# A chunked delta-rule scan: the first inversion's input copied in two parts, the scans' output matmuls split another way

## The chip, the cores and the metric

The kernel runs on one NeuronCore of a Trainium2 chip. TensorE (PE) multiplies matrices out of SBUF into PSUM banks; VectorE (DVE), ScalarE (ACT) and GpSimd (POOL) work elementwise; SyncE (SP) and ScalarE issue the DMAs. Each engine runs its own instructions in a fixed order and waits on semaphores for the others. The metric is device microseconds of one execution; the median of three runs counts.

## The reference

The model is a trunk of two layers over 512 positions of 1024 channels in float32, each followed by a gated convolutional FFN. Layer 0 is a spatial-gating MLP, layer 1 an RWKV-7 time mixer with 16 heads of 64 channels. The change lies in the time mixer. Its core is a recurrence per head:

```python
def step(state, inp):
    r_t, w_t, k_t, v_t, a_t, b_t = inp
    sa = jnp.einsum('bhvk,bhk->bhv', state, a_t)
    state = (state * w_t[:, :, None, :]
             + sa[..., None] * b_t[:, :, None, :]
             + v_t[..., None] * k_t[:, :, None, :])
    y_t = jnp.einsum('bhvk,bhk->bhv', state, r_t)
    return state, y_t
...
y = wkv7_scan(r_h, decay, k_h, v_h, -kk, kk * a_h)
mean = jnp.mean(y, -1, keepdims=True)
var = jnp.mean(jnp.square(y - mean), -1, keepdims=True)
y = ((y - mean) * lax.rsqrt(var + GN_EPS)).reshape(B, S, D)
y = y * ln_w.astype(f32) + ln_b.astype(f32)
bonus = jnp.sum(r_h * k_h * r_k.astype(f32), -1, keepdims=True) * v_h
return ((y + bonus.reshape(B, S, D)) * g) @ w_o
```

## The kernel before

The whole kernel is one program: the gating MLP, an FFN, the time mixer, an FFN, a final norm. Dense products are three float32r matmuls of 128x128 by 128x512 each (high by high, high by low, low by high; `mm3`, lines 325 to 327). The change touches only the time mixer, `rwkv_main`.

The recurrence is not run step by step. The 512 positions are cut in 8 chunks of 64. Heads go in pairs, two heads of 64 channels on 128 partitions: 8 pairs, in two groups `g` of four. Three kinds of work are chained:

**Pairs** (`pairs`, `decay`, `operands`, `products`). For pair `p` they work out decays and scaled operands and the 64x64 matrices of every chunk. Of these, `a` and `r` (tile `ar`) and the masked products (tile `lq`: a strictly lower one, M, and an inclusive one, N, per head) are stored by DMA in a DRAM buffer `std[g]`, laid out per chunk as 128 partitions by pair by RW = 320 columns. Before, the columns are `r` (0 to 64), then for head 0 first the block [a; M] and then N (64 to 192), and the same for head 1 (192 to 320); the store of `ar` takes three DMAs per pair on SP's queue, that of `lq` three per half. A further product is copied into `ti[g]`: the triangular matrices to be inverted.

**Inversions** (`invert(g)`). For a group the 32 unit triangular matrices (4 pairs by 8 chunks) of both heads are inverted at once in blocks of 32. Their input `x` is copied from `ti[g]` by quarter (`Q`), transposed by VectorE (`turn`, line 1051), eliminated in 30 steps on VectorE (lines 1058 to 1072), transposed back, and finished by small matmuls (lines 1090 and 1093). For `g == 0` the copy is four ScalarE copies of 32 partitions by all 1024 elements (line 1046) when pairs 0 to 3 are done. For `g == 1` it is ScalarE copies of 24 of the 32 matrices (line 1046) at one step and VectorE copies of the last 8 (line 1044) at the next.

**Scans** (`scan(g)`). For each chunk `c`, with tile `vu` holding the values `v` in one half of the partitions and the state in the other, a chunk has three parts, and yields after each:

- part A: the right side `us` = [a; M] by [state; v] (line 1301, 128 rows), copied to `wt` (line 1304); the first half of the output `e`, `r` by the state (line 1305, 64 rows); the decayed state `s0` on GpSimd;
- part B: the solve, `ti` by `wt` (line 1314, 64 rows), copied over the state's half of `vu` (lines 1315 and 1316);
- part C: the next state's product (line 1321, 128 rows, not in the last chunk), added to `s0` into the next chunk's `vu` (line 1325); the second half of the output, N by [solution; v] (line 1326, 128 rows), then two ScalarE copies of `e` into `y` (line 1329).

After every second chunk `finish` is started: it is the head norm of 128 positions (squares, a sum, a reciprocal root with GpSimd's power, a product, four transposes, line 1363, and a scaling on VectorE, line 1366). It is a generator, stepped once in each part (`self.step(late)`); what is left of it is drained (`yield from late`) before the next one takes its place. The last one of a scan is handed on (`left`).

`weave` sets the order around it. It steps a main generator (pairs, later a scan), and with each of its yields adds a rate to a sum; each time the sum reaches 1 it takes one step of `fill`: dense products of the projections, the gates and the output projection (`project`), two of its operands in a step. The rates are in `RATES` on line 33, 0.66 for the first scan and 0.72 for the second. A second generator, the inversion, is stepped beside. `issue_after` queues instructions of an engine behind a given one; within these limits a planner with its own cost model sets each engine's order.

After the second scan comes its end: the last `finish`, with steps of `fill` written out between its steps:

```python
rest, left = left.pop(), None
next(rest)
for _ in range(2):
    next(fill)
next(rest)
next(fill)
next(rest)
with tc.issue_after(self.last(mybir.EngineType.PE)):
    next(fill)
```

There `project` for group 1 gives no work until the last `finish` has gated its outputs.

## Time and profile before

| what | us |
|---|---|
| median of 3 runs | 1244.65 (1244.2 to 1246.1) |
| the profiled execution | 1245.55 |
| its span | 1243.7 |
| TensorE busy | 1226.8 (99%) |
| VectorE busy | 851.1 (68%) |
| ScalarE busy | 633.1 (51%) |
| GpSimd busy | 81.4 (7%) |
| mean granted TensorE clock | 0.996 of full speed |

The times of the profile are those of one execution. A row of a timeline gives the start in us from the span's beginning, the busy time, engine, line, operation, the tiles written and read, the shape, and the number of instructions that were merged in the row; in brackets the idle time of the engine just before and what ended it. Matmuls are pipelined: the time that a batch takes of TensorE is the distance of its start to the next one's start. The pairs run from about 570 to 720 us, the scans from 725 to 845 us.

### The profile page before, as it was taken

How to read it: one execution, taken by the hardware profiler on the slowest of the kernel's cores; microseconds unless marked ns; L12 is line 12 of the kernel's file. 1: busy time of each engine (PE TensorE's matmuls, PEld its weight loads, DVE VectorE, ACT ScalarE, POOL GpSimd, SP SyncE). 2: the span in 40 equal slices, each digit the busy share in tenths (PEclk: the TensorE clock that was granted, in tenths of full speed). 3: DMA queues.
4: the chain of work that ended last, by engine and by line, in shares of the span. 5: the costliest groups of instructions: out<-in, count | busy, mean ns of one | idle time of the engine just before them, and what ended most of it. 6: DMA issues, size and time to landing. Idle time of an engine off the chain costs nothing.

```text
span 1243.7 us, 19411 instructions
## 1 busy us (share of the span) xinstructions
PE 1226.8 (99%) x7535; PEld 1000.2 (80%) x7535; DVE 851.1 (68%) x1418; ACT 633.1 (51%) x1089; POOL 81.4 (7%) x106
## 2 busy tenths in 40 slices
PE   9999999999999999999999999999999999999997
PEld 6878888888888888877887777778888888888886
DVE  5566578888876454675899698776777777872323
ACT  6544455555554343466787667424544444543232
POOL 1100200000000001000000013222000000000000
PEclk9999999999999999999999899999999999999999
DMA  7232457887556776326888797654223223333332
GB/s 273 94 105 82 132 180 246 246 249 241 192 172 193 220 226 196 109 81 182 220 242 237 188 280 233 219 171 135 85 102 102 90 97 102 97 88 104 97 93 81
DMA packets 125133, 201.65 MB, mean 162 GB/s; under 512 B 39857, under 2 KB 63153, under 8 KB 125041
## 3 DMA queue, kind: packets, MB, share of 16 engines
q10 hardware_dynamic: 38976, 112.87, 29.5%
q1 hardware_dynamic: 86064, 87.54, 22.6%
q8 instruction: 59, 0.97, 0.3%
q14 instruction: 34, 0.27, 0.1%
HBM read 152.93 MB, written 47.45 MB: 161 GB/s over the span
## 4 chain that ended last, share of the span: by engine, by line
PE 91%; DVE 4%; DMA 3%; ACT 1%; issue 0%; SPq 0%; POOL 0%; DVEq 0%; POOLq 0%; ACTq 0%
PE mm L325 9%; PE mm L327 9%; PE mm L326 9%; PE aux L325 6%; PE aux L326 6%; PE aux L327 6%; PE e L325 6%; PE e L326 6%; PE us L325 6%; PE e L327 6%; PE us L327 6%; PE us L326 6%; PE us L1314 1%; PE aux L973 1%; PE aux L988 1%; PE us L1321 1%
## 5 line engine op out<-in xcount | busy, mean ns | idle before, releaser
L237 ACT CAST w<-w 128x512 fp32r<-128x512 f32 x340 | 206.5, 611 | 359.8 <-PE aux L327 92.6
L238 DVE TENSOR_TENSOR w<-w,w 128x512 fp32r<-128x512 f32 x340 | 230.5, 680 | 180.2 <-ACT w L237 179.6
L325 PE MATMUL mm<-mxh,w 128*128 128x512 f32 x408 | 167.9, 412 | 2.7 <-DVE rt L885 2.6
L327 PE MATMUL mm<-mxh,w 128*128 128x512 f32 x408 | 161.1, 395 | 0.0
L326 PE MATMUL mm<-mxl,w 128*128 128x512 f32 x408 | 160.6, 394 | 0.0
L325 PEld LDWEIGHTS mm<-mxh,w 128*128 128x128 f32 x408 | 77.0, 189 | 22.8 <-DVE rt L885 3.3
L327 PEld LDWEIGHTS mm<-mxh,w 128*128 128x128 f32 x408 | 77.0, 189 | 17.1 <-issue 0.8
L326 PEld LDWEIGHTS mm<-mxl,w 128*128 128x128 f32 x408 | 77.1, 189 | 16.2 <-issue 1.7
L575 ACT ACTIVATE cv<-z,par 128x512 f32<-128x512 f32 x88 | 71.7, 817 | 26.5 <-DVE z L573 21.2
L325 PE MATMUL aux<-mxh,w 128*128 128x512 f32 x216 | 84.5, 391 | 0.0
L325 PE MATMUL us<-mxh,w 128*128 128x512 f32 x216 | 84.5, 391 | 0.0
L327 PE MATMUL aux<-mxh,w 128*128 128x512 f32 x216 | 84.2, 390 | 0.0
L326 PE MATMUL aux<-mxl,w 128*128 128x512 f32 x216 | 84.1, 389 | 0.0
L326 PE MATMUL us<-mxl,w 128*128 128x512 f32 x216 | 84.1, 389 | 0.0
L327 PE MATMUL us<-mxh,w 128*128 128x512 f32 x216 | 84.1, 389 | 0.0
L354 POOL TENSOR_TENSOR ss<-ss,sq 128x512 f32<-128x512 f32 x24 | 31.7, 1323 | 761.1 <-ACT sq L352 761.1
L325 PE MATMUL e<-mxh,w 128*128 128x512 f32 x208 | 81.4, 391 | 0.0
L326 PE MATMUL e<-mxl,w 128*128 128x512 f32 x208 | 81.1, 390 | 0.0
L327 PE MATMUL e<-mxh,w 128*128 128x512 f32 x208 | 81.0, 389 | 0.0
L576 DVE SCALAR_TENSOR_TENSOR cv<-z,par,cv 128x512 f32<-128x512 f32 x88 | 66.0, 752 | 19.5 <-ACT cv L575 19.5
L577 DVE SCALAR_TENSOR_TENSOR cv<-z,par,cv 128x512 f32<-128x512 f32 x88 | 66.0, 752 | 2.9
L325 PEld LDWEIGHTS aux<-mxh,w 128*128 128x128 f32 x216 | 40.5, 188 | 9.0 <-issue 0.5
(1113 smaller groups left out, 2555.2 us busy)
## 6 DMA issues: line engine op xcount, KB each, us to landing
w<-in_wup ACTq DMA_DIRECT2D x88, 512.0 KB, 3.7
w<-in_wdn ACTq DMA_DIRECT2D x32, 512.0 KB, 3.7
st<-std SPq DMA_DIRECT2D x15, 640.0 KB, 6.6
w<-wkd ACTq DMA_DIRECT2D x16, 512.0 KB, 5.1
w<-wvd ACTq DMA_DIRECT2D x16, 512.0 KB, 5.1
w<-wod ACTq DMA_DIRECT2D x16, 512.0 KB, 4.2
w<-in_wdn ACTq DMA_DIRECT2D x16, 384.0 KB, 3.3
w<-in_wsu ACTq DMA_DIRECT2D x8, 512.0 KB, 3.7
```

The lines of the kernel that those rows point to most:

```text
L237: nc.scalar.copy(hi[r, :n], src)
L238: (lo_eng or nc.vector).tensor_tensor(lo[r, :n], src, hi[r, :n].bitcast(F32), ALU.subtract)
L325: mm(acc, wh, xh, start=first, stop=False)
L326: mm(acc, wh, xl, start=False, stop=False)
L327: mm(acc, wl, xh, start=False, stop=last)
L354: nc.gpsimd.tensor_tensor(self.ss, self.ss, self.sq, ALU.add)
L575: nc.scalar.activation(c, z[:, 2:], AF.Identity, scale=cw(2, i), bias=self.p("conv_b", l * 44 + i))
L576: nc.vector.scalar_tensor_tensor(c, z[:, 1:T + 1], cw(1, i), c, ALU.mult, ALU.add)
L577: nc.vector.scalar_tensor_tensor(c, z[:, 0:T], cw(0, i), c, ALU.mult, ALU.add)
L973: nc.tensor.matmul(qs[hd][:, c - ch.start, :], bk[H[hd], c, C * hd:C * hd + P], ar[H[hd], c, :], start=True, stop=True)
L988: nc.tensor.matmul(qs[hd][:, c, :], bk[H[hd], c, C * hd:C * hd + P], dg[H[hd], c, :], start=True, stop=True)
L1314: nc.tensor.matmul((us, ux)[hd][H[hd], 1, i, :], ti[g][H[hd], i, c, :], wt[H[hd], i, :], start=True, stop=True)
```

## The change

Three things are changed, all of them in `rwkv_main`.

**The input of the first inversion.** The split of the second inversion (24 matrices by ScalarE, then 8 by VectorE) is used for both. The first inversion is created before the pairs' first weave, and its first step (the ScalarE copies of the matrices of pairs 0 to 2) is taken as soon as pair 2 is done, from inside that weave (`opened`). Its second step (VectorE's copies, the transpose) comes where the whole copy stood.

**The output's halves.** `e` is now first [r; N] by [state; v] (128 rows, `both(i, hd, 1)`), in part A, and then N by the solution (64 rows), in `ready`. `ready` is called in part B of the next chunk, behind the solve's copies and queued behind the solve's matmuls, or at once in the last chunk. Its ScalarE copies into `y` go with it. For that, `std` has another layout: `r` stands in the rows of `a`, and N's columns of the solution's rows stand at 0 to 64. `ar` is stored in two DMAs of 128 columns instead of three of 64.

**The norms.** Since `y` is complete one chunk later, `finish` for two chunks starts in part B of the chunk after the next pair's begin, and the last but one is drained after the scan's last chunk.

```diff
-            for rows, o, q in ((h0, C, 0), (h1, 3 * C, 0), (slice(0, P), 0, C)):
-                nc.sync.dma_start(std[g][:, rows, i, o:o + C].rearrange("c p t -> p c t"), ar[rows, :, q:q + C])
+            for rows, o in ((h0, 3 * C), (h1, C)):
+                nc.sync.dma_start(std[g][:, rows, i, o:o + P].rearrange("c p t -> p c t"), ar[rows])
...
-                for hd, o, n, q in ((0, P, P + C, C), (1, C, P, 0), (1, 2 * P, C, P + C)):
+                for hd, o, n, q in ((0, 0, P + C, C), (1, 3 * C, P, 0), (1, 0, C, P + C)):
...
-            cut = 24 * g
-            for us in (slice(0, cut), slice(cut, 32))[1 - g:]:
+            for us in (slice(0, 24), slice(24, 32)):
                 for rows, cols in Q:
-                    if us.start and g == 1:
+                    if us.start:
                         V.tensor_copy(x[rows, us], tg[rows, us, cols])
                     else:
                         S.copy(x[rows, us], tg[rows, us, cols])
-                if g == 1 and us.start == 0:
+                if us.start == 0:
                     yield
...
-            y = None
+            y = past = ready = None
...
                 def both(i, hd, n):
-                    o = C + P * hd + n * C
+                    o = C + P * (1 - hd) + n * C
                     return st[i][:, o:o + C]
...
-                batch(lambda i, hd, n: nc.tensor.matmul(e[H[hd], 0, i, :], st[i][H[hd], 0:C], vu[H[hd], hd, i, :],
+                batch(lambda i, hd, n: nc.tensor.matmul(e[H[hd], 0, i, :], both(i, hd, 1), vu[:, hd, i, :],
                                                         start=i == 0, stop=False, skip_group_check=True), lead)
...
                 V.tensor_copy(vu[h0, 0], us[h0, 1])
                 S.copy(vu[h1, 1], ux[h1, 1])
+                if ready is not None:
+                    ready(self.last(mybir.EngineType.PE))
                 self.step(late)
+                if c % 2 == 0 and ready is not None:
+                    yield from late
+                    late = finish(g, c // 2 - 1, past)
                 yield
...
-                batch(lambda i, hd, n: nc.tensor.matmul(e[H[hd], 0, i, :], both(i, hd, 1), vu[:, hd, i, :],
-                                                        start=False, stop=True, skip_group_check=True), lead)
-                for hd in range(2):
-                    S.copy(y[H[c % 2], :, hd, :], e[H[hd], 0])
+
+                def ready(lead, c=c, e=e, st=st, vu=vu, y=y):
+                    batch(lambda i, hd, n: nc.tensor.matmul(e[H[hd], 0, i, :], st[i][H[hd], 0:C], vu[H[hd], hd, i, :],
+                                                            start=False, stop=True, skip_group_check=True), lead)
+                    for hd in range(2):
+                        S.copy(y[H[c % 2], :, hd, :], e[H[hd], 0])
+
+                past = y
+                if last:
+                    ready(None)
                 self.step(late)
                 yield
-                if c % 2 == 1:
-                    yield from late
-                    late = finish(g, c // 2, y)
-            left.append(late)
+            yield from late
+            left.append(finish(g, c // 2, y))
...
-        self.weave(until(main, lambda: 3 in done), None, fill, *RATES[0], ktiles=STEPS[0])
         inv = invert(0)
+
+        def opened(gen):
+            for _ in gen:
+                if 2 in done and not begun:
+                    begun.append(next(inv))
+                yield
+
+        begun = []
+        self.weave(opened(until(main, lambda: 3 in done)), None, fill, *RATES[0], ktiles=STEPS[0])
```

## The prediction

> **What bounds the kernel now.** I read the page first, then a table by stretches, then the timelines of single engines. The page:
>
> ```profile
> span 1243.7 us, 19411 instructions
> PE 1226.8 (99%) x7535; PEld 1000.2 (80%) x7535; DVE 851.1 (68%) x1418; ACT 633.1 (51%) x1089; POOL 81.4 (7%) x106
> ...
> PEclk9999999999999999999999899999999999999999
> ...
> PE 91%; DVE 4%; DMA 3%; ACT 1%; issue 0%; SPq 0%; POOL 0%; DVEq 0%; POOLq 0%; ACTq 0%
> ```
>
> TensorE is busy for all but 1243.7 − 1226.8 = 16.9 us, and the change neither adds nor removes a matmul. So time can come only from four places: idle TensorE, a slower granted clock, bubbles between matmuls of different shape, and new idle time. The clock row has one digit below nine, around 690 to 720 us. Cut finer (columns: stretch, its length, busy PE, PEld, DVE, ACT, POOL with counts, granted clock, DMA share, GB/s):
>
> ```profile
> 694.00:697.00 3.00, 0.72 (x5) 0.25 (x3) 2.83 (x10) 1.42 (x4) 0.00 (x0) 1.00 0.91 222
> ...
> 698.00:700.00 2.00, 1.81 (x15) 1.27 (x15) 2.00 (x2) 0.89 (x2) 0.00 (x0) 0.50 0.60 181
> 700.00:705.00 5.00, 5.00 (x44) 4.31 (x40) 1.48 (x1) 3.41 (x6) 0.00 (x0) 0.52 0.09 33
> ```
>
> TensorE idles 2.28 us in the first stretch and then runs at half clock; that loses about 2.0 × 0.50 + 5.0 × 0.48 = 3.4 us. The TensorE timeline gives the gap and its releaser:
>
> ```profile
> 694.31 0.40 PE L327 MATMUL mm<-mxh,w 128*128 128x512 f32 x1
> 696.99 0.50 PE L325 MATMUL mm<-mxh,w 128*128 128x512 f32 x1 [2.28 <-DVE rt L885]
> ```
>
> It waited for a VectorE instruction of line 885. VectorE's timeline shows what that one queued behind:
>
> ```profile
> 652.57 1.22 DVE L911 TENSOR_TENSOR_SCAN sq<-cst,sq 128x512 f32<-128x512 f32 x1
> 656.56 2.02 DVE L1051 STREAM_TRANSPOSE li<-ix 128x1024 f32<-128x1024 f32 x1 [2.77 <-ACT ix L1046]
> ...
> 696.25 0.68 DVE L885 TENSOR_TENSOR rt<-mm,v 128x512 f32<-128x512 f32 x1
> ...
> 714.75 1.18 DVE L1044 COPY ix<-ti 32x256 f32<-32x256 f32 x4
> ```
>
> Between the transpose at 656.56 and line 885 no row of this timeline carries an idle time: VectorE is the bound of that stretch, and it enters it 2.77 us late because ScalarE copies the first inversion's input (ix).
>
> **Part 1, the early copy.** The 2.77 us hole goes if three quarters of the copy are made earlier. In their place VectorE gets four copies of 32x256, which the second inversion already has: 1.18 us. Net −1.6 us for everything behind VectorE. But ScalarE must make four copies of 32x768 one pair earlier, and these are priced by the second inversion's as well (grouped by line; the second pair of numbers is busy us and mean ns):
>
> ```profile
> L1046 ACT COPY ix<-ti 32x768 f32<-32x768 f32 x4 | 3.3, 829 | 0.0
> ```
>
> The old ones were issued just behind the decay of the pair after, so I expect the new ones around 630 to 640 us:
>
> ```profile
> 631.32 0.72 ACT L690 ACTIVATE mt<-h,par 128x512 f32<-128x512 f32 x1 [0.96 <-DVE mxl L238]
> ...
> 633.25 0.41 ACT L802 CAST l<-w 128x256 fp32r<-128x256 f32 x1 [0.70 <-PE e L899]
> ...
> 640.05 0.63 ACT L913 ACTIVATE sq<-kn 128x512 f32<-128x512 f32 x1
> ```
>
> ```profile
> 641.64 1.05 PE L923 MATMUL e<-cst,sq 128*128 128x128 f32 x8
> 642.74 0.17 DVE L925 TENSOR_SCALAR n<-e 128x8 f32<-128x8 f32 x1 [1.10 <-PE e L923]
> ```
>
> ScalarE's square (L913, done 640.68) feeds L923 (641.64) and through it VectorE, which already idles 1.10 us there; the slack is 0.96 us. Queued behind the copies are L913, the exponentials and the mixes that feed the dense fill. If all 3.3 us come ahead of L913, VectorE starts 3.3 − 0.96 = 2.3 us later and the sum is −2.77 + 1.18 + 2.3 = +0.7. If the copies fall into the holes of 0.96 and 0.70 us and the rest into the slack, it is −1.6. I take −1.0, nearer the hidden end because holes and slack add to 2.6 of the 3.3 us.
>
> The gap at 694 does not shrink with it in my main case: TensorE's own earlier waits in the stretch are on the same late engines, so both sides of that wait move together, and the half clock stays.
>
> **Part 2, the split output.** Per chunk the kernel issues three batches of us, one of the old solution, and two for the output. From the first scan:
>
> ```profile
> 738.39 0.69 PE L1321 MATMUL us<-vu,cbt 128*64 128x64 f32 x16
> 738.91 0.64 PE L1326 MATMUL e<-vu,st 128*64 128x64 f32 x16
> 739.48 0.50 PE L325 MATMUL mm<-mxh,w 128*128 128x512 f32 x1
> ...
> 740.37 0.69 PE L1301 MATMUL us<-vu,st 128*64 128x64 f32 x16
> 740.98 0.68 PE L1305 MATMUL e<-vu,st 64*64 64x64 f32 x16
> 741.60 0.50 PE L325 MATMUL mm<-mxh,w 128*128 128x512 f32 x1
> ...
> 745.59 0.69 PE L1321 MATMUL us<-vu,cbt 128*64 128x64 f32 x16
> ```
>
> A 128-row batch followed by a 128-row one takes 738.91 − 738.39 = 0.52 us; followed by a 64-row one 740.98 − 740.37 = 0.61. Today the output's first half (64 rows, L1305) follows 128 rows, and its second half (128 rows, L1326) follows 128 rows. Afterwards the first half has 128 rows behind 128 rows, and the second has 64 rows behind the solve, which has 64 rows too. One change of shape per chunk goes: 16 × 0.09 = −1.4 us. Bounds: 0, if dense fill is planned in between, and −1.4.
>
> The second half used to stand behind the state product (L1321), where it covered VectorE's update of the values:
>
> ```profile
> 739.18 0.87 DVE L1325 TENSOR_TENSOR vu<-us,wt 64x256 f32<-64x256 f32 x2
> ```
>
> That update ends at 740.05 and L1301 starts at 740.37, behind three dense matmuls. Without the 0.57 us of L1326 (738.91 to 739.48) TensorE comes there at 739.80 and waits 0.25 us, unless fill takes the place. It now covers the copies behind the solve instead, where the traced chunk has more fill. Bounds: 0 and, for the 7 chunks of each scan with a state product, 14 × 0.25 = +3.5; I take +0.5, as fill may be planned into most of the holes. The output copies on ScalarE move with their matmuls, behind the solve's copy.
>
> A chunk's state buffer is read one part longer. Its reload waits for the last reader on SP's queue (the load is 6.6 us on the page's list of issues):
>
> ```profile
> 739.59 0.42 SPq L1246 DMA_DIRECT2D st<-std  x1
> ```
>
> Issued at 739.59 it lands near 746.2. A chunk is 745.59 − 738.39 = 7.2 us long, and this buffer is used two chunks after the L1301 of 740.37, so near 754.8. Released behind the next solve, some 4 us later, it still has 4 us of cover: nothing. With that cover gone, L1301 would wait for the rest of the 6.6 us. The store of ar in two DMAs instead of three takes eight issues from SP's queue; no compute wait quoted here is on them: nothing.
>
> **Part 3, norms later.** finish() starts one chunk part later, so the last but one norm is not used up inside the scan: each scan gets one more turn of the weave. At rates 0.66 and 0.72 the first scan takes 16 steps of fill instead of 15 (25 turns for 24) and the second 18 instead of 17 (26 turns for 25; 25 × 0.72 stays a rounding error below 18). Two steps more are gone before the end of the second scan, and that end counts on exactly four:
>
> ```profile
> 840.17 0.50 PE L325 MATMUL mm<-mxh,w 128*128 128x512 f32 x1
> ...
> 843.02 0.28 PE L325 MATMUL us<-sg,gwh 128*128 128x256 f32 x1
> ...
> 844.93 0.40 PE L325 MATMUL mm<-mxh,w 128*128 128x512 f32 x1
> ...
> 846.35 0.60 PE L1363 MATMUL aux<-cst,y 128*128 128x128 f32 x4
> 846.70 0.48 PE L325 MATMUL mm<-mxh,w 128*128 128x512 f32 x1
> ...
> 848.17 0.49 PE L325 MATMUL mm<-mxh,w 128*128 128x512 f32 x1
> ```
>
> Two steps stand at 840.17, one at 844.93 (1.42 us), one at 846.70 (1.47); at 848.17 the second projection begins. Two steps less there and two more in the scans: the latter cost 2.9 us, less the holes that they fill. In the end phase the first transposes of the norm could go at 845.3, since their input is done then:
>
> ```profile
> 844.58 0.69 DVE L1357 TENSOR_TENSOR y<-y,gr 128x512 f32<-128x512 f32 x1
> ```
>
> So the phase shortens by 846.35 − 845.3 = 1.0 us, and 0.35 us of transposes (price of L1363's four) move into it from the scan, under cover. The transposes' four VectorE instructions (1.13 us) come with them, into the idle time before the squares' sum:
>
> ```profile
> 838.26 1.13 DVE L1366 SCALAR_TENSOR_TENSOR rt<-aux,par,rt 128x128 f32<-128x128 f32 x4
> ...
> 841.72 0.69 DVE L1347 TENSOR_REDUCE gs<-ysq 128x8 f32<-128x512 f32 x1 [2.33 <-ACT ysq L1342]
> ```
>
> Sum +2.9 − 1.0 − 0.35 = +1.5, less the holes filled in the scans, which can be at most the idle time of
>
> ```profile
> 720.00:800.00 80.00, 77.38 (x1282) 58.27 (x1283) 67.91 (x157) 51.07 (x101) 21.60 (x27) 1.00 0.84 263
> ```
>
> 2.6 us. Bounds +1.5 and −1.1; I take +1.0, because most of that idle time lies in the first scan, which gets only one of the two steps, at its end.
>
> **The sum** is −1.0 − 1.4 + 0.5 + 1.0 = −0.9 us against the profiled execution's 1245.55 (span 1243.7 and 1.85 around it): 1244.65. That execution lies 0.9 above the median of the runs, 1244.65, so for a median I forecast 1243.7. What a measurement here can tell from no change is 0.2%, 2.5 us.
>
> **The rivals.**
>
> *The half clock goes.* If TensorE's gap at 694 falls well under 2.28 us, 3.4 us more are won: 1240.3. For it: the 2.6 us of idle time from 720 to 800, which lie in pieces, went by at a granted clock of 1.00. Against it: TensorE is early there by its own work, and arrives still earlier if its waits on ScalarE go.
>
> The Trainium skill (TensorE: Matmul & The Clock Gate, "What's actually happening") lets the clock drop only after an idle window of some 3.4 us. Here it fell after 2.28 us, so the trace does not bear out that length; by the rule the gap would not be the cause, and shortening it would not win the 3.4 us.
>
> *All covers hold.* Copies in ScalarE's holes (−1.6), no hole behind the state product (0), the end phase at 0: −1.6 − 1.4 = −3.0: 1241.6. For it: fill is planned by readiness. Against: VectorE is busy 67.9 of 80 us in the first scan, so its updates come late.
>
> *The end phase breaks: slower.* With two steps of fill gone, TensorE's idle time between 840 and 848 becomes one gap as long as the one at 694, and half clock follows as it did there: +1.5 instead of +1.0, and +3.4: 1247.6. It decides from a gap of about 2.28 us. Against: openings (843.02 to 844.93) and transposes stand in the middle and would cut it in two.
>
> *The cover behind the state product is missed: slower.* +3.5 instead of +0.5: 1246.7, and past the bound if VectorE is late in part 1 as well (+0.7 instead of −1.0): 1248.4. For it: VectorE's 67.9 of 80 us; against it: the matmuls that moved are now fill for the wait before.
>
> That the change does nothing at all, because the early copies are planned where the old ones were, is within the main case: 0 instead of −1.0 in part 1.
>
> **How the numbers follow.** Main case 32%, its own range 1242.2 to 1247.1, the 0.2% around 1244.65. Half clock goes 26%, all covers hold 14%, end phase 16%, cover missed 12%, half of it beyond the 0.2%. Faster is the second and third: 40%; same 32 + 6 = 38%; slower 16 + 6 = 22%. The range reaches below the half-clock case, which can meet the third (1240.3 − 2.1 = 1238.2), and above to the slower ones, 1248.4; I leave a little out at the bottom: 1238.4 to 1248.4.
>
> **What would show it.** Part 1: in the changed kernel the wait of VectorE's first transpose on ix gone, four ix copies of 32x768 before 645 us, and L925's idle of 1.10 us not above 2. The half clock: the clock row without a digit under nine near 700. Part 2: the 128-row output batch taking 0.52 and not 0.61 us with what precedes it, and L1301's waits on VectorE not over 2 us in total. Part 3: between the last state output and the second projection two steps of fill, not four, and about 1.5 us of idle TensorE. I am wrong if VectorE's hole merely moves forward to 641, if a second half-clock stretch appears, or if the order in which the planner puts everything between 640 and 850 us turns out so different that these stretches can't be matched.

## The result and the profile after

The changed kernel takes 1257.15 us in the median (1254.96 to 1258.54, four runs) against 1244.43 for the kernel before (1243.8 to 1246.1, four runs): ratio 1.0097, 95% interval 1.0083 to 1.0111. It is slower by some 12 us; I had forecast 1243.7 within 1238.4 to 1248.4. The profiled execution took 1256.69. Line numbers behind the edit shift: before's L1051 is now L1050, L1044 L1043, L1062 L1061, L1301 L1300, L1314 L1313, L1325 L1329, L1363 L1371; the output's second half is L1332 and its first still the line behind the right side, L1304.

The head of the page after:

```profile
span 1254.7 us, 19418 instructions
...
PE 1228.2 (98%) x7535; PEld 1002.1 (80%) x7535; DVE 850.9 (68%) x1422; ACT 632.9 (50%) x1089; POOL 80.6 (6%) x106
```

TensorE does the same 7535 matmuls in 1228.2 us instead of 1226.8, and is idle for 1254.7 − 1228.2 = 26.5 us instead of 16.9. So of the 11.0 us by which the span is longer, 9.6 are new waits; the 1.4 us more that the same matmuls are busy go with a lower mean clock, 0.992 instead of 0.996. The table by stretches of the kernel after (columns as in the prediction) says where:

```profile
694.00:697.00 3.00, 3.00 (x13) 2.06 (x11) 2.83 (x10) 1.41 (x4) 0.00 (x0) 1.00 0.88 233
697.00:702.00 5.00, 0.35 (x3) 0.04 (x1) 4.87 (x5) 3.96 (x6) 0.00 (x0) 0.76 0.67 176
702.00:709.00 7.00, 7.00 (x50) 5.61 (x51) 0.00 (x0) 2.59 (x6) 0.00 (x0) 0.50 0.24 75
764.00:768.00 4.00, 4.00 (x46) 3.71 (x43) 1.75 (x6) 3.73 (x5) 0.00 (x0) 0.57 0.12 46
720.00:800.00 80.00, 74.13 (x1276) 56.74 (x1272) 66.29 (x158) 51.37 (x100) 18.10 (x23) 0.98 0.79 240
```

The gap near 695 is there again, but TensorE is idle for 4.65 us of 697 to 702. The clock falls inside that gap already (0.76 in the mean of 697 to 702), and the whole of 702 to 709 runs at half clock. A second half-clock stretch stands at 764 to 768. From 720 to 800 TensorE is busy for 74.13 us where it was 77.38. TensorE's timeline after gives the marks:

```profile
701.96 0.80 PE L325 MATMUL mm<-mxh,w 128*128 128x512 f32 x1 [4.65 <-DVE rt L885]
...
731.08 0.34 PE L1300 MATMUL us<-rb,mxh 128*64 128x64 f32 x4
...
763.13 0.69 PE L1300 MATMUL us<-vu,st 128*64 128x64 f32 x16 [1.94 <-issue]
...
857.99 0.60 PE L1371 MATMUL aux<-cst,y 128*128 128x128 f32 x4
860.17 0.73 PE L325 MATMUL mm<-mxh,w 128*128 128x512 f32 x2 [1.58 <-ACT mxh L1212]
```

and the timeline of before has for the second of them:

```profile
725.79 0.34 PE L1301 MATMUL us<-rb,mxh 128*64 128x64 f32 x4
```

The first scan starts 731.08 − 725.79 = 5.3 us late; 0.7 us of this stand already ahead of the early copies (the scale of the pair before, L913, at 622.95 instead of 622.23). The last transposes, at 846.35 before, come at 857.99, 11.6 us late. So 5.3 us are lost ahead of the scans and 6.3 from there to the last transposes; 0.6 come back behind them, where less fill is left.

For the wait of 1.94 us at 763 the profile names no releaser ("issue"). VectorE's timeline shows what the right side there had to wait for, the update of the values (L1329), which stands behind transposes of the second inversion and ends at 763.03:

```profile
760.83 1.49 DVE L1050 STREAM_TRANSPOSE ix<-li 128x256 f32<-128x256 f32 x3
762.18 0.85 DVE L1329 TENSOR_TENSOR vu<-us,wt 64x256 f32<-64x256 f32 x2
```

The first loss shows in VectorE's timeline after:

```profile
650.22 1.17 DVE L1043 COPY ix<-ti 32x256 f32<-32x256 f32 x4
651.43 2.10 DVE L1050 STREAM_TRANSPOSE li<-ix 128x1024 f32<-128x1024 f32 x1
653.39 0.67 DVE L951 SCALAR_TENSOR_TENSOR ta<-ta,rb 128x512 f32<-128x512 f32 x1
...
656.70 0.70 DVE L977 TENSOR_TENSOR lq<-aux,cst 128x512 f32<-128x512 f32 x1
...
659.04 0.24 DVE L1061 SCALAR_TENSOR_TENSOR li<-li 128x30 f32<-128x30 f32 x1
...
697.70 1.91 DVE L1050 STREAM_TRANSPOSE ix<-li 128x1024 f32<-128x1024 f32 x1
699.48 1.89 DVE L1050 STREAM_TRANSPOSE li<-li 128x1024 f32<-128x1024 f32 x1
701.25 0.66 DVE L885 TENSOR_TENSOR rt<-mm,v 128x512 f32<-128x512 f32 x1
```

Against before, from VectorE's timeline of that kernel:

```profile
651.37 0.69 DVE L977 TENSOR_TENSOR lq<-aux,cst 128x512 f32<-128x512 f32 x1
...
658.66 0.21 DVE L1062 SCALAR_TENSOR_TENSOR li<-li 128x30 f32<-128x30 f32 x1
```

The hole of 2.77 us ahead of the opening transpose is gone, as planned. But copies and transpose now stand ahead of the pair's operands (L951 and on), for 3.2 us, and L925, ahead of them all, starts at 644.81 instead of 642.74, behind ScalarE's late scale. So the masked product (L977) comes at 656.70 instead of 651.37. The elimination has nothing from it: it starts at 659.04, 0.4 us later than before, and ends with the closing transposes at 697.70, as before. The third folded input (L885), ahead of these transposes at 696.25 before, is now behind both.

Inside the scans the batches changed their neighbours as planned. TensorE's timeline after, one chunk:

```profile
739.78 0.69 PE L1300 MATMUL us<-vu,st 128*64 128x64 f32 x16
740.30 0.64 PE L1304 MATMUL e<-vu,st 128*64 128x64 f32 x16
...
741.92 0.68 PE L1313 MATMUL us<-wt,ti 64*64 64x64 f32 x16
742.43 0.28 PE L1332 MATMUL e<-rb,mxh 64*64 64x64 f32 x4
...
744.60 0.69 PE L1325 MATMUL us<-vu,cbt 128*64 128x64 f32 x16
745.21 0.50 PE L325 MATMUL mm<-mxh,w 128*128 128x512 f32 x1
```

740.30 − 739.78 is 0.52 us, and 742.43 − 741.92 is 0.51. But the state product, which had an output batch of its own shape behind it before (0.52), is now followed by dense fill and takes 745.21 − 744.60 = 0.61. Over a scan, the usual times from a batch's start to the next start add up as follows, for the right side, the output's first half, the solve, the state product and the output's second half: before 0.61 + 0.61 + 0.61 + 0.52 + 0.57 = 2.92 us a chunk, after 0.52 + 0.57 + 0.51 + 0.62 + 0.56 = 2.78. So 0.14 us a chunk are won, in the 14 chunks with a state product an estimated 2 us.

### The profile page after: what moved, and what is told of

Its sections match the earlier page's. It is cut to its first block, busy times and chain, and to the rows that moved or that the text cites. A ratio compares the mean times of both kernels' runs of the same rounds, so it can differ in the third digit from the quotient of the medians.

```text
span 1254.7 us, 19418 instructions
## 1 busy us (share of the span) xinstructions
PE 1228.2 (98%) x7535; PEld 1002.1 (80%) x7535; DVE 850.9 (68%) x1422; ACT 632.9 (50%) x1089; POOL 80.6 (6%) x106
```

## The experiments

All ratios are to the kernel before, timed on the same chip in the same series, each with its 95% interval; 0.001 is 1.24 us.

### 1 and 2: each half of the change alone

The early copy alone:

```
             x = blocks("ix")
-            cut = 24 * g
-            for us in (slice(0, cut), slice(cut, 32))[1 - g:]:
+            for us in (slice(0, 24), slice(24, 32)):
...
+        self.weave(opened(until(main, lambda: 3 in done)), None, fill, *RATES[0], ktiles=STEPS[0])
```

> The kernel before with only the first inversion's input copied early (three of its four quarters on ScalarE inside the first weave, the rest on VectorE); scans and stores as before. Theory A (the copy costs what the trace shows ahead of the scans: the first scan matmul stands 5.3 us later, TensorE's wait on the input transposes' eviction grows from 2.3 to 4.7 us): 1249.5 us, between 1248 and 1251.5, with the wait near 697 us about 4.7 us long. Rival (the stores' new layout or the shifted order of all the work does it): 1244.4 us, within 1 us of the kernel before. My prediction's own step: 1243.4 us.

Measured: 1253.94 us, 1.0069 (1.0051 to 1.0086). The rest of the change, with that part undone:

> The changed kernel with the first inversion's input copied as before: the split output, its deferred second half, the norms a part later and the stores' layout stay. Theory A (two independent costs, 5.3 us of the copy and some 6 to 7 us inside the scans and behind them): 1251 us, between 1249.5 and 1252.5, first scan matmul within 1 us of the kernel before. Rival (all of it comes from the scans' edit, the delay ahead of them included): 1257 us. If the two parts hurt each other: below 1249.

Measured: 1248.47 us, 1.0025 (1.0015 to 1.0034). The two add up: 0.69% + 0.25% = 0.94% against 0.97% for the whole. Both times lie outside what I had expected, the first above and the second below. So some seven tenths of the loss are the early copy, more than the 5.3 us I had read from the start of the scans: in the first run's trace the first scan starts at 731.63, 5.8 us late, and 3.7 us more are lost from there to the last transposes (855.93). That trace has the wait of 4.65 us too, ending at 701.79, with half clock over all of 702 to 709, and a second stretch of half clock inside the first scan:

```profile
734.00:740.00 6.00, 4.74 (x42) 4.02 (x44) 5.06 (x14) 1.83 (x5) 0.16 (x1) 0.72 1.06 329
```

Its six executions differ with the clock: from 1251.02 us at a mean granted clock of 0.996 to 1257.61 at 0.991.

### 3 and 4: inside the scans, first look

Halves exchanged, with the new layout, but the second half left in part C and the norms as before:

```
-            for rows, o, q in ((h0, C, 0), (h1, 3 * C, 0), (slice(0, P), 0, C)):
+            for rows, o in ((h0, 3 * C), (h1, C)):
...
-                batch(lambda i, hd, n: nc.tensor.matmul(e[H[hd], 0, i, :], st[i][H[hd], 0:C], vu[H[hd], hd, i, :],
+                batch(lambda i, hd, n: nc.tensor.matmul(e[H[hd], 0, i, :], both(i, hd, 1), vu[:, hd, i, :],
                                                         start=i == 0, stop=False, skip_group_check=True), lead)
```

> The kernel before with the stores' layout of the changed one and the output's two halves exchanged (128 rows first, 64 rows second), but the second half where it was, in part C right behind the state product, and the norms as before. Theory B (the loss in the scans is the deferral and what hangs on it, the shape change alone still saves its 0.09 us in each of 16 chunks): 1243 us, between 1242 and 1244.2. Rival (the layout, with its reload and its two stores, or the new order that it gives, costs by itself): 1247 us or more.

Measured: 1243.72 us, 0.9990 (0.9982 to 0.9999). The layout costs nothing; the loss in the scans is in the deferral and the norms. The time is about what I had put on the change of shape, but it doesn't come from there. In this run the 64-row batch stands behind the 128-row state product, which now pays for it:

```profile
736.56 0.69 PE L1321 MATMUL us<-vu,cbt 128*64 128x64 f32 x16
737.18 0.68 PE L1326 MATMUL e<-vu,st 64*64 64x64 f32 x16
```

In the order of the sum above a chunk takes 0.52 + 0.57 + 0.61 + 0.62 + 0.61 = 2.93 us, against 2.92 before. What gains the 1.2 us no run isolates.

That the norm, begun in part B, has VectorE wait for GpSimd was my first guess (the wait of y on GpSimd's gr came to 9.2 us in 8 places in the changed kernel, from 2.3 in 3):

```
-                if c % 2 == 0 and ready is not None:
-                    yield from late
-                    late = finish(g, c // 2 - 1, past)
...
                 self.step(late)
+                if c % 2 == 0 and c:
+                    yield from late
+                    late = finish(g, c // 2 - 1, past)
+                past = y
                 yield
```

> The second run's kernel (split output, second half behind the next solve, copy as before) but with each norm begun at the end of part C of that chunk instead of in its part B, so that its steps fall on parts A, B and C in the order of the kernel before, three parts later. Theory C (the scans lose because the norm begun in part B has VectorE wait for GpSimd's power: 9.2 us of such waits in 8 places against 2.3 us in 3 before): 1246.5 us, between 1245 and 1248, and the waits back to about 2 to 3 us. Rival (the deferral itself costs, by the product that no longer stands behind the state product): the same as the second run within 1 us, about 1251.

Measured: 1250.59 us, 1.0038 (1.0024 to 1.0052), no better than the second run. But the waits that were to go stayed: 6.5 us in 6 places, from 7.5 in 8 in the second run. So this run does not test the theory. Beginning the norm still later also takes 17 and 19 steps of fill in the scans, and the profiled end had TensorE at half clock from 852 to 858 us.

### 5 and 6: what of the early copy costs

The early copies on GpSimd instead of ScalarE:

```
-                        S.copy(x[rows, us], tg[rows, us, cols])
+                        (S.copy if g else G.tensor_copy)(x[rows, us], tg[rows, us, cols])
```

> The first run's kernel (early copy alone) with the three early quarters copied on GpSimd instead of ScalarE; the last quarter stays on VectorE. Theory A1 (the four ScalarE copies of 0.83 us put the scale at line 913 from 640.05 to 642.8 us, and everything behind it): the scale back at 640 us, the wait on the third folded input back to about 2.5 us, 1245.5 us, between 1244 and 1247.5. Rival A2 (VectorE's order does it: copies and the transpose at 650 to 653.4 us, ahead of the pair's operands): the scale back at 640 us, but the masked product still near 655 us instead of 651.4, the wait 4 us or more, 1251 to 1254 us.

Measured: 1253.55 us, 1.0082 (1.0063 to 1.0101). It doesn't tell A1 from A2, because moving the copies hurt VectorE. GpSimd's timeline and VectorE's in that run:

```profile
631.36 4.51 POOL L1045 COPY ix<-ti 32x768 f32<-32x768 f32 x4 [9.59 <-ACT ti L978]
```

```profile
631.38 1.35 DVE L691 SCALAR_TENSOR_TENSOR mt<-h,omu,mt 128x512 f32<-128x512 f32 x1
632.65 1.30 DVE L944 TENSOR_TENSOR ar<-kn,gt 128x512 f32<-128x512 f32 x1
...
635.11 1.31 DVE L951 SCALAR_TENSOR_TENSOR ta<-ta,rb 128x512 f32<-128x512 f32 x1
636.34 0.68 DVE L953 TENSOR_TENSOR ss<-ss,key 128x512 f32<-128x512 f32 x1
```

While GpSimd copies, from 631.36 to 635.87, each of the four VectorE operations takes about 1.3 us; the next one takes 0.68. The four lose 2.5 us, nearly what ScalarE's scale had been late (640.05 to 642.93). The scale comes at 647.00 here; 4.4 us of that are older than the copies, as the pair before is late by as much (626.67 instead of 622.23). The sixth run leaves the copies and changes one place, the closing transposes:

```
-            turn(z.rearrange("p u t -> p t u"), tt)
+            with ExitStack() as behind:
+                if g == 0:
+                    behind.enter_context(tc.issue_after(self.folded))
+                turn(z.rearrange("p u t -> p t u"), tt)
```

(`self.folded` is the last instruction of line 885; the second transpose is wrapped in the same way.)

> The first run's kernel (early copy alone) with the inversion's two closing transposes (1.9 us each on VectorE, from 697.5 us) ordered behind the third folded input (line 885), which stands behind them at 701.1 us there. Theory A3 (those 3.8 us are what makes TensorE wait 4.8 us, and that wait brings the half clock of 9 us and more behind it): the wait near 697 us about 1 us, no half clock at 700 to 710 us, 1246.5 us, between 1245 and 1248.5. Rival (the pairs' work is late anyway, and the transposes, now later, hold up the block products as much): 1251 us or more.

Measured: 1247.75 us, 1.0030 (1.0018 to 1.0042). VectorE's timeline, then TensorE's and the table by stretches:

```profile
698.20 0.69 DVE L885 TENSOR_TENSOR rt<-mm,v 128x512 f32<-128x512 f32 x1
698.80 2.06 DVE L1050 STREAM_TRANSPOSE ix<-li 128x1024 f32<-128x1024 f32 x1
```

```profile
698.94 0.50 PE L325 MATMUL mm<-mxh,w 128*128 128x512 f32 x1 [0.99 <-DVE rt L885]
```

```profile
702.00:709.00 7.00, 7.00 (x103) 5.53 (x102) 2.25 (x4) 6.04 (x11) 0.00 (x0) 1.00 0.61 175
```

The wait is 0.99 us, the clock full, and 6.2 us are back by the medians, 4.9 by the ratios. This theory stands: more than half of what the early copy costs is that two transposes passed one instruction for which TensorE waits.

What is left lies inside the scans. The first scan starts at 724.92, 0.9 us ahead of the kernel before, but it takes 3.0 us longer from there to the last transposes (848.48). One wait is most of that, and ScalarE's timeline shows what the copy that TensorE waits for stands behind:

```profile
762.26 0.69 PE L1326 MATMUL us<-vu,cbt 128*64 128x64 f32 x16 [2.51 <-ACT vu L1321]
```

```profile
758.63 1.04 ACT L1103 COPY ti<-li 32x1024 f32<-32x1024 f32 x1 [2.69 <-DVE li L1050]
...
761.84 0.37 ACT L1321 COPY vu<-us 64x256 f32<-64x256 f32 x1
```

In the kernel before, the same copy of the solution into vu stands at 757.57, and the inversion's copy into ti behind it, at 763.66. So a second time a piece of the inversion has passed an instruction for which TensorE waits; no run puts that one back, and what it is worth in the median is not shown.

### 7 and 8: deferral or norms

The second half deferred for the even chunks alone, norms as before (the edit is shown against the changed kernel):

```
                 S.copy(vu[h1, 1], ux[h1, 1])
-                if ready is not None:
+                if c % 2 == 1:
                     ready(self.last(mybir.EngineType.PE))
...
-                if last:
-                    ready(None)
+                if c % 2 == 1:
+                    ready(lead)
```

> The third run's kernel (halves exchanged, all in place) with the second half put behind the next solve for the even chunks only; the odd chunks keep theirs behind the state product, and the norms begin where they did before. Theory C1 (the deferral itself loses the cover behind the state product): half of the 4.75 us between the second and the third run, 1246.1 us, between 1245 and 1247.2. Rival C2 (the loss is the norms' lateness, the deferral is free): 1243.7 us, within 0.8 us of the third run.

Measured: 1246.95 us, 1.0019 (1.0011 to 1.0028). Nothing deferred, but the norms begun in part B of the next chunk:

```
                 S.copy(vu[h1, 1], ux[h1, 1])
                 self.step(late)
+                if c % 2 == 0 and c:
+                    yield from late
+                    late = finish(g, c // 2 - 1, past)
```

> The third run's kernel (halves exchanged, all in place) with each norm begun in part B of the next chunk, as in the changed kernel, and nothing deferred. Theory C2 (the norms' lateness is the loss in the scans and at the end): 1248.2 us, between 1247 and 1249.5, with TensorE waiting about 1.8 us behind the last transposes. Rival C1 (the deferral is): 1243.9 us, within 0.8 us of the third run; if the end alone suffers, 1245.5.

Measured: 1246.22 us, 1.0017 (1.0008 to 1.0025). Both cost against the third run's 0.9990: the even chunks' deferral 0.29% or 3.6 us, the later norms 0.27% or 3.4 us. Neither is free, so neither theory alone is right, and by these ratios they cost less together than their sum (the second run has both at 0.35% over the third). The waits of y on GpSimd's gr go with the norms and not with the deferral: 2.4 us in the seventh run, 6.5 in the eighth, 2.3 in the third. So the first guess is not ruled out for the norms' share. The eighth run's TensorE timeline has the wait at the end that the changed kernel has:

```profile
849.19 0.73 PE L325 MATMUL mm<-mxh,w 128*128 128x512 f32 x2 [1.58 <-ACT mxh L1213]
```

### 9 and 10: ScalarE or VectorE's order

Early copies added on ScalarE, the old ones kept, so that VectorE's order stays:

```
+            if g == 0:
+                for rows, cols in Q:
+                    S.copy(x[rows, 0:24], tg[rows, 0:24, cols])
+                yield
             cut = 24 * g
```

> The kernel before with the three early quarter copies added on ScalarE inside the first weave, and the four whole copies kept where they were, which write the same input again: ScalarE has the early copies, while VectorE's written order stays the one of the kernel before but for one place (the opening transpose one row later). Theory A1 (the early copies on ScalarE delay the pairs' scale and with it everything): the scale at line 913 near 642.8 us, 1249 us or more. Theory A2 (VectorE's order does it, ScalarE's lateness alone is absorbed): the scale at 642.8 us too, but the masked products and the third folded input within 1.5 us of before, 1245 us, between 1244 and 1246.5.

Measured: 1246.11 us, 1.0010 (1.0002 to 1.0018). ScalarE's scale is nearly as late as in the changed kernel (642.49 for 642.93), but VectorE far less: its masked product is 1.8 us behind the kernel before instead of 5.3, and the third folded input, 1.7 us late, is still ahead of the closing transposes. ScalarE's timeline, then VectorE's:

```profile
642.49 0.63 ACT L913 ACTIVATE sq<-kn 128x512 f32<-128x512 f32 x1
```

```profile
653.13 0.68 DVE L977 TENSOR_TENSOR lq<-aux,cst 128x512 f32<-128x512 f32 x1
...
697.97 0.68 DVE L885 TENSOR_TENSOR rt<-mm,v 128x512 f32<-128x512 f32 x1
699.39 1.98 DVE L1055 STREAM_TRANSPOSE ix<-li 128x1024 f32<-128x1024 f32 x1
```

So the early copies on ScalarE cost 1.2 us (0.2 to 2.2) of the first run's 8.6, by a run that makes the old copies too; the rest comes with VectorE's copies and the new order. The tenth run is the sixth without VectorE's copies:

```
-                    if us.start:
+                    if us.start and g == 1:
                         V.tensor_copy(x[rows, us], tg[rows, us, cols])
```

> The sixth run's kernel (early copy alone, closing transposes behind the third folded input) with the last quarter copied on ScalarE as well, so that VectorE has no input copies and the opening transpose stands behind the third pair's masked product instead of ahead of its operands. Theory A2 (what is left of the loss, 3.4 us, comes from the copies and the transpose ahead of the pair's operands on VectorE): 1244.7 us, between 1243 and 1246, masked product back near 652.5 us. Theory A1 (it comes from ScalarE's early copies): 1247.7 us, within 0.8 us of the sixth run.

Measured: 1247.73 us, 1.0017 (1.0007 to 1.0028). By the ratio it is 1.6 us better than the sixth run, by the median the same, and the intervals overlap: whether the opening transpose ahead of the pair's operands costs by itself stays open. In the trace the masked product is back at 653.32 and the first scan starts at 723.19, 1.7 us ahead of the sixth run's; but the wait for vu is there again, 2.50 us up to 760.53, with half clock behind it to 764.

### 11, 12 and 16: the fill, and the whole change mended

The eighth run with fewer steps of fill:

```
-RATES = ((1.9, 2), (1.9, 6, 2.2), (0.66, 2, 1.15), (0.72, 2), (1.2, 6, 2.2))
+RATES = ((1.9, 2), (1.9, 6, 2.2), (0.62, 2, 1.15), (0.68, 2), (1.2, 6, 2.2))
```

> The eighth run's kernel (nothing deferred, norms begun in the next chunk's part B) with the two scans' fill rates lowered from 0.66 and 0.72 to 0.62 and 0.68, so that the scans take 15 and 17 fill steps again, as before, where the later norms made it 16 and 18. Theory D (the wait of 1.8 us at the end is missing fill, not the norm itself): the wait near 847 us down to 0.5 us or less, 1244.7 us, between 1243.8 and 1245.6. Rival (the last norms' own lateness sets the end): 1246.2 us, within 0.5 us of the eighth run.

Measured: 1246.06 us, 1.0011 (1.0001 to 1.0020). The wait at the end is gone from the trace, but the time hardly follows: 0.7 us, inside the intervals. So the wait was the symptom that I could see. Part of what the later norms cost besides stands at their transposes: TensorE waits 2.3 us there for y in two places, and 0.5 in the third run. The rest is not located. The changed kernel with both mends, the sixth run's and this one:

> The changed kernel whole, with two mends: the closing transposes behind the third folded input, as in the sixth run, and the scans' fill rates at 0.62 and 0.68, so that 15 and 17 fill steps are taken. If the two causes add up with the rest: 1257.2 less 6.2 less 1.6, 1249.4 us, between 1248 and 1251. Rival (other waits take their place, as the order is planned anew): 1252 us or more.

Measured: 1247.28 us, 1.0017 (1.0008 to 1.0025): 10 us of the 12 are back, with the early copy and the deferral both still in. With the transposes' mend alone:

> The changed kernel whole with the closing transposes alone put behind the third folded input, fill rates as in the changed kernel. The twelfth run, with both mends, gave back 10 us where the single runs had 6.2 and less than 1. If the transposes' place carries that: 1248 us, within 1 us of the twelfth run; if the fill steps carry more in the whole change than alone: 1250 us or more, with a wait of 1.8 us at the end.

Measured: 1249.22 us, 1.0035 (1.0023 to 1.0048). The transposes' place carries 7.7 us of the whole, 0.62%, and the two steps of fill, by the twelfth run's ratio, 2.2. The trace has the 7.7 us where they should be: the first scan starts at 723.19 instead of 731.08, and takes 127 us to the last transposes as in the changed kernel.

### 13, 14 and 15: the same wait in the kernel before

Before, the third folded input starts at 696.25, though its product (L883, issued at 692.30 for 1.02 us) is done by then. It is put ahead of the last five elimination steps:

```
+                    if g == 0 and j == 26:
+                        for _ in range(2):
+                            yield
+                    with ExitStack() as behind:
+                        if g == 0 and j == 26:
+                            behind.enter_context(tc.issue_after(self.folded))
                         V.tensor_tensor(q, a, b, ALU.mult)
```

> The third run's kernel (halves exchanged, nothing deferred, no early copy) with the third folded input (line 885) put ahead of the first inversion's last five elimination steps on VectorE: in the kernel before it starts 3 us after its product is done, and TensorE waits 2.45 us for it. Theory E (that wait sets the end of this stretch, and the half clock follows it in some executions): the wait at 1 us or less, 1241.8 us, between 1240.5 and 1243. Rival (the later elimination steps hold up the block products as much): 1243.7 us, within 0.8 us of the third run, or slower.

> The kernel before with that one edit alone (the third folded input ahead of the last five elimination steps). Theory E: 1242.6 us, between 1241.3 and 1243.8. Rival: 1244.5 us, within 0.8 us of the kernel before, or slower.

> The seventh run's kernel (second half deferred for the even chunks, norms as before) with the third folded input ahead as in the thirteenth run. It tells how much of the seventh run's loss of 3.2 us against the third is the half clock ahead of the scans, by chance of its executions: if the deferral itself costs, it stays 2.5 us or more above the thirteenth run; if it was the half clock, 1 us or less.

Measured: 1248.81 us, 1.0027 (1.0017 to 1.0038); 1248.74 us, 1.0033 (1.0020 to 1.0045); 1252.04 us, 1.0055 (1.0042 to 1.0067). The fifteenth is 0.28% above the thirteenth, as the seventh above the third: the deferral's 3.5 us are its own, not those of a half clock ahead of the scans. The tables by stretches of the thirteenth and of the fifteenth run, in this order, show where:

```profile
720.00:800.00 80.00, 76.85 (x1300) 57.85 (x1298) 66.67 (x149) 50.27 (x99) 22.94 (x27) 1.00 0.78 246
```

```profile
720.00:800.00 80.00, 74.29 (x1231) 56.34 (x1232) 64.33 (x144) 49.32 (x97) 21.77 (x27) 1.00 0.79 232
```

TensorE loses 2.6 us more there, in the first scan, in waits of 1 us and less (right side, solve, mixes); which of them is first I can't say. The surprise is that the other two are slower than what they were made from. TensorE's timeline of the fourteenth:

```profile
696.67 0.50 PE L325 MATMUL mm<-mxh,w 128*128 128x512 f32 x1 [0.61 <-DVE rt L885]
...
851.72 1.22 PE L325 MATMUL mm<-mxh,w 128*128 128x512 f32 x2 [2.12 <-ACT mxh L1219]
```

The wait fell from 2.28 to 0.61 us, and a wait of 2.12 us came up at the end, in this execution with half clock (0.51 over 851 to 858). The two added turns of the weave take two steps of fill: 65 are used ahead of the first scan instead of 63, counted as the program is built, and 97 instead of 95 ahead of the end. The changed kernel has 97 there too.

### 17 and 18: the two steps given back

```
         for n, _ in enumerate(inv):
-            next(fill)
+            if n >= 2:
+                next(fill)
```

> The thirteenth run's kernel (halves exchanged, third folded input ahead of the last five elimination steps) with the two fill steps taken back that its two extra turns of the weave had used up ahead of the scans (65 used by then instead of 63), so that the end has as many left as in the kernel before. Theory D (fill used early is missing at the end): the waits at 809 and 849 us gone, and then the shorter wait for the folded input pays: 1241.5 us, ratio to the kernel before between 0.9955 and 0.9985. Rival (the elimination's lateness costs as much as the wait gave): ratio 0.999 to 1.001.

> The fourteenth run's kernel (the kernel before with the third folded input ahead of the last five elimination steps) with its two fill steps taken back in the same way. Theory D and E: the end wait of 2.4 us gone, ratio to the kernel before 0.9965 to 0.9995. Rival: 1.000 or more.

Measured: 1242.17 us, 0.9980 (0.9970 to 0.9990), and 1243.64 us, 0.9991 (0.9982 to 0.9999). No wait is left at the end of either. Two steps of fill, used ahead of the first scan and missing behind the second, had cost 5.8 and 5.2 us. TensorE's timeline of the seventeenth run, and its stretch behind the gap:

```profile
696.17 0.50 PE L325 MATMUL mm<-mxh,w 128*128 128x512 f32 x1 [0.59 <-DVE rt L885]
```

```profile
702.00:709.00 7.00, 7.00 (x83) 5.29 (x82) 3.10 (x6) 6.19 (x9) 0.00 (x0) 1.00 0.76 201
```

The seventeenth, halves exchanged and the folded input ahead, beats both kernels: 2.5 us below the one before and 15 below the changed one.

## Why the prediction was wrong

**Part 1 (early copy), put at −1.0 within −1.6 to +0.7; measured +8.6.** The step that failed is "Net −1.6 us for everything behind VectorE". It moved everything behind the hole forward in one piece, in the order of the old trace. But the order is planned: an input that is ready earlier is placed earlier, here ahead of the operands that TensorE waits for, and the elimination starts no sooner for it. What I had priced with care, ScalarE's 3.3 us ahead of L913, came out inside my bounds: the scale was 2.9 us late and VectorE's L925 2.1, 0.7 of each standing ahead of the copies already. That leaves 1.4 of the 2.3 us that I had as the worst case, and the ninth run puts the price of the early copies on ScalarE at 1.2. The hole did not move to 641, the first thing that I said would prove me wrong (VectorE idles 1.20 us there, before 1.10). The other two did come: a second half-clock stretch, and another order between 640 and 850 us. I had named them and given them neither a price nor a chance.

**"The gap at 694 does not shrink, and the half clock stays."** It doubled, from 2.28 to 4.65 us, because two transposes of 1.9 us passed one instruction of 0.68. The sixth and sixteenth runs show that this alone carries 4.9 us in the early copy and 7.7 in the whole change. Why the planner put them ahead is not isolated; the product that the folded input waits for (L883) comes 2.6 us later than before, at 694.90 instead of 692.30. What else the new order did, the sixth run's trace shows in one place: 2.51 us of waiting in the first scan for a copy that a piece of the inversion had passed.

**Part 2.** The shape change, −1.4, was counted on too few batches: I had left out what follows the state product and the second half. By the batches' times it is 0.14 us a chunk, some 2 us, instead of 0.09. No run has it alone: the third run's −1.2 us looks like it, but its batches add up to 2.93 us a chunk against 2.92 before, so the agreement is luck. The layout costs nothing, as I had said, and no wait of TensorE in the changed kernel's scans is put down to the load of the state buffer. The deferral, +0.5 with +3.5 as the bound for all chunks, was mis-sized: 3.6 us with only the even chunks deferred. I had priced one wait at one place, 0.25 us behind each state product; what came is spread over the first scan, where VectorE was busy for 67.9 of 80 us, and only partly at that place: in the fifteenth run 0.7 of the 5.7 us that TensorE idles from 720 to 800 are waits of the right side, in the changed kernel 1.9 of 5.9.

**Part 3, +1.0.** The steps of fill (16 and 18) and "about 1.5 us of idle TensorE" came: 1.58. Between the last output and the second projection stand three steps, not the two forecast (18 matmuls of 512 columns from 851.86, where before had 24). The price was mis-sized: the later norms cost 3.4 us against the third run, over my bound of 1.5. Giving the steps back returned 0.7 us when nothing was deferred and 2.2 in the whole change, so the rest lies in the norms' own lateness, of which only TensorE's waits for y are located.

**The rivals.** "The cover is missed" (1246.7) was nearest for the scans: the longest wait, 1.94 us at 763, is of its kind, and half clock came behind it; the others lie elsewhere. "The end phase breaks" came as far as its gap, and no half clock followed it in the changed kernel, though it did in the fourteenth run, with 2.12 us. "The half clock goes" had the right lever with the wrong price: in the eighteenth run the gap is down to 0.58 us, the profiled execution has no half clock, and the gain is 1.1 us (0.1 to 2.2), not 3.4. That price came from one profiled execution. The third run's profiled execution has the same gap, and no half clock behind it:

```profile
697.30 0.50 PE L325 MATMUL mm<-mxh,w 128*128 128x512 f32 x1 [2.28 <-DVE rt L885]
```

```profile
702.00:709.00 7.00, 7.00 (x100) 5.41 (x99) 1.98 (x3) 6.84 (x12) 0.00 (x0) 1.00 0.57 153
```

## What to carry to other kernels

Where a planner sets each engine's order, an input that is ready earlier is first of all a new order: ask which instruction of the path the freed work will pass, and price that, before counting the hole that it fills. Independent work that covers waits is a stock: whatever draws a step of it early, an extra turn of a loop included, is paid for where it was meant to stand. And a loss that one profiled execution shows by a lower clock is to be priced by several executions.

## What the runs showed of the hardware

- What a batch of 16 small matmuls takes of TensorE depends on its neighbours: 0.51 to 0.52 us where a batch with as many rows follows, and 0.56 to 0.57 for that second batch ahead of dense matmuls; 0.61 to 0.62 where it stands alone, ahead of a batch with another number of rows or of dense matmuls. These are the usual values in the scans of the kernel before, the third run and the changed kernel.
- A GpSimd copy holds up VectorE: beside four copies of 32x768 in 4.51 us, four VectorE operations on two inputs took 1.30 to 1.35 us where the next took 0.68. The Trainium skill (SBUF — State Buffer, "SBUF: two separate sides") has the two engines share one pair of ports as an exclusive lock, also against a VectorE operation with two SBUF inputs; the trace agrees, with one operation lengthened by some 0.6 us for each copy.
- The half clock is not tied to the length of a gap alone. Behind a gap of 2.28 us it came in the profiled execution of before and not in that of the third run; behind 4.65 us it came in both traces; behind 1.94 us at 763 of the changed kernel it came (0.57 over 764 to 768), and with 2.12 us at the end of the fourteenth run (0.51 over 851 to 858); behind 1.58 us at the changed kernel's end and in the eighth run it did not. How long it lasts comes in steps of 3.4 us: 6.8 us in the kernel before (697.9 to 704.8), 10.2 and 3.4 in the changed one (699.6 to 709.9 and 764.4 to 767.9), 6.8 in the fourteenth run (851.0 to 857.9). In the changed kernel it set in 2.3 us after TensorE fell idle, in the kernel before 0.9 us after TensorE had started again. The Trainium skill (TensorE: Matmul & The Clock Gate, "What's actually happening") has the clock drop after an idle window of some 3.4 us, in windows that run on by themselves. That the same gap has it in one execution and not in another agrees with the second half, and so do the steps of 3.4 us; drops behind 2.28 and 1.94 us don't agree with a whole window of idle time.
